# A two-layer hybrid decoder: S5 tables mirrored about their middle, modulation pages spread over the gates, small inputs joined, unread products in TensorE's waits

## The chip, the cores and the metric

The kernel runs on one core of a Trainium2 chip. The time is the device time of one execution in microseconds (us); the figure for a kernel is the median of its runs. Per instruction the trace gives start and duration on each engine: TensorE (PE, with its weight loads as PEld), VectorE (DVE), ScalarE (ACT), GpSimd (POOL), and SyncE (SP), which here only issues transfers.

## What is computed

The reference is a decoder trunk of two layers for 256 tokens of width 1024, in f32. Conditioning `c` gives six modulation vectors per layer; four token mixers run in parallel on slices of one input projection, are gated and merged; then comes a mixture of 16 experts with two chosen per token.

```python
def reference(x, c, positions, ada_w, ada_b, ...):
    c_act = jax.nn.silu(c)
    for l in range(DEPTH):
        mod = (c_act @ ada_w[l] + ada_b[l]).reshape(bsz, 6, 1, d)
        shift1, scale1, gate1, shift2, scale2, gate2 = (mod[:, i] for i in range(6))
        h = rmsnorm(x, mix_norm_g[l]) * (1.0 + scale1) + shift1
        u, q, k, v, iq, ik, iw, rg_x, rg_g, rw_f = _split(h @ w_in[l], IN_WIDTHS)
        # o_s5 (complex diagonal scan), o_dsa (top-k attention), o_rg (RG-LRU), o_rw (RWKV-7)
        up = jnp.einsum('btnw,nwd->btnd', branches, branch_w[l])
        gates = jax.nn.sigmoid(h @ gate_w[l] + gate_b[l]).reshape(bsz, seq, N_BRANCH, d)
        mixed = jnp.einsum('btnd,btnd->btd', gates, up) @ out_w[l]
        x = x + gate1 * mixed
        h2 = rmsnorm(x, ffn_norm_g[l]) * (1.0 + scale2) + shift2
        x = x + gate2 * moe(h2, router_w, router_b, exp_w1[l], exp_w3[l], exp_w2[l])
    return rmsnorm(x, final_norm_g)
```

The S5 scan needs the cosine and sine of 0 to 255 multiples of an angle for each state; these are the "tables".

## The kernel before

Weights come as pages of 128 x 2048 f32 (1 MB) through SyncE's queue, in one list written out ahead (`order`): the modulation pages of group 0 of layer 0 and `x`, then per layer the weights of the mixers, the pages of the fill plan, the output projection and the experts. A page is requested as soon as a buffer is free, from a ring of 5 and from a pool of 15 pages that work tiles share.

A weight that is multiplied in f32 is split into a high and a low part by `halves` (L598 to L601: ScalarE copies, VectorE subtracts), and `three` (L626 to L646) makes three matmuls of it; their line in the trace is L633 or L635.

The work of a layer is written as Python generators that a loop steps in turn (L1706 to L1757): `rwkv`, `others` (DSA, then S5, then RG-LRU) and, in layer 0, `s5_tables`. Beside them it steps `fill`, once the tables are there: two steps per chain step, later 1 and 3. `fill` (L1284 to L1309) follows `fill_plan` (L178 to L190), a string of 20 marks: a digit is a gate (48 matmuls of 128x256, then a tanh on ScalarE, L1309), a letter is the merge of a branch (L1311 to L1340). Ahead of each gate stand modulation pages: three in layer 0, whose list is groups 1 and 2 of the layer and then group 0 of the next, and two in layer 1. A scheduler then orders each engine's instructions by when they can run; an engine runs its own in order.

`ada` (L467 to L497) multiplies one modulation page. For groups marked `EARLY`, (0,0) and (1,0), TensorE does it (L480) into one of three PSUM banks tagged "acc", kept until the group's eighth page. For the others ScalarE scales the first page (L486) and VectorE adds each later one in four operations (L488). The addend `ada_b` has four rows of 512; GpSimd clears a 128x512 tile (L473) and ScalarE's queue loads the rows into it (L474). With the eighth page the sum is turned and stored as shift, scale and gate (`mod_values`, L516; `ada_rows` with L513).

`s5_tables` (L719 to L749) doubles the tables on GpSimd: from n entries come the next n, for n of 1, 2, 4 to 128, with six operations of 128 x 8n each (L731 to L736) and the doubled angle in five small ones (L740 to L744). Layer 0's runs as a chain at the start; layer 1's is stepped through in layer 0's `experts` (L1570 to L1654, at L1632 to L1634), between the fifth and the sixth of eight expert pairs.

`experts` gathers the tokens of a pair (L1532, L1536), multiplies by w1 and w3 (L1592), forms the SwiGLU (L1499, L1500), turns the result (`turn`, copied by ScalarE at L1511), multiplies by w2 (L1614) and adds the weighted result back in `combine` (L1563, L1564). `route` (L1432 to L1494) ranks the experts on VectorE and counts the tokens of each in five small matmuls (`pk`, L1457 to L1461).

Of the kernel before, what the change touches and what calls it, by code (L numbers as in the profile page):

```python
# [13 lines left out]
I32 = mybir.dt.int32  # L14
# [43 lines left out]
NMAT = _o  # L58

# [87 lines left out]
def _emit(ctx, tc, I, out):  # L147
# [30 lines left out]
    def fill_plan(l):  # L178

        groups = [(l, 1), (l, 2)] + ([(l + 1, 0)] if l + 1 < L else [])  # L180
        adas = [("ada", ll, g, kt) for ll, g in groups for kt in range(KT)]
        plan, k, ng, seen = [], 0, len(groups), [0] * 4
        for c in PLAN:
            if c.isdigit():
                plan += adas[k:k + ng] + [("gate", l, seen[int(c)], int(c))]
                k += ng
                seen[int(c)] += 1
            else:
                plan.append(("br", l, "abcd".index(c)))
        return plan  # L190
# [72 lines left out]

    def row(name, n):
        return bass.AP(tensor=I[name].tensor, offset=I[name].offset, ap=[[0, P], [1, n]])

    cols = []
    for l in range(L):
        c = ct(f"cols{l}", [P, NCOL])
        nc.scalar.dma_start(c, I["cols"][l])  # L270
        cols.append(c)
# [5 lines left out]
    pos_i = ct("pos_i", [P, 2], I32)  # L277
    nc.scalar.dma_start(pos_i, I["pos"])
    freq = ct("freq", [P, 48])
    nc.scalar.dma_start(freq, row("freq", 48))  # L280
    rtb = ct("rtb", [P, NE])
    nc.scalar.dma_start(rtb, row("router_b", NE))
    rtw = ct("rtw", [P, KT, NE])
    nc.scalar.dma_start(rtw, I["router_w"])
# [182 lines left out]
    def ada(l, g, kt):  # L467


        early = (l, g) in EARLY  # L470
        if kt == 0:
            b = M.take([P, 512])
            G.memset(b, 0.0)  # L473
            nc.scalar.dma_start(b[0:P:32, :], I["ada_b"][l, g])  # L474
            part[l, g] = b, pt("acc", [P, 512]) if early else M.take([P, 2048])
        b, p = part[l, g]
        w = get(("ada", l, g, kt))
        if early:
            for j in range(4):
                PE.matmul(p[32 * j:32 * j + 32, :], csil[:, kt, :], w[:, 512 * j:512 * j + 512],  # L480
                          start=kt == 0, stop=kt == KT - 1)
        else:
            for j in range(4):
                js = slice(512 * j, 512 * j + 512)
                if kt == 0:
                    S.activation(p[:, js], w[:, js], AF.Copy, scale=csil[:, kt, 0:1])  # L486
                else:
                    V.scalar_tensor_tensor(p[:, js], w[:, js], csil[:, kt, 0:1], p[:, js], op0=OP.mult, op1=OP.add)  # L488
        done(("ada", l, g, kt))
        if kt == KT - 1:  # L490
            if not early:
                a, p = p, pt("acc", [P, 512])
                for j in range(4):
                    PE.matmul(p[32 * j:32 * j + 32, :], ones_f[:, 0:32], a[:, 512 * j:512 * j + 512], start=True, stop=True)
                M.free(a)
            V.tensor_tensor(b, p, b, OP.add)
            mod_values(l, g, b)  # L497
# [10 lines left out]
    def ada_rows(o, r, j0):  # L508

        for j in range(2):  # L510
            p = pt("mx", [P, 512])
            q = slice(32 * (j0 + j), 32 * (j0 + j) + 1)
            PE.matmul(p, ones_f[q, :], r[q, :], start=True, stop=True)  # L513
            S.activation(o[:, 512 * j:512 * j + 512], p, AF.Copy, scale=0.5)
# [204 lines left out]
    def s5_tables(l, tabs):  # L719

        cs, sn = M.take([P, 8, T]), M.take([P, 8, T])
        tt = M.take([P, 8, P])
        G.memset(cs[:, :, 0:1], 1.0)
        G.memset(sn[:, :, 0:1], 0.0)
        ec, es = cs5[:, l], sn5[:, l]
        n = 1
        while n < T:
            t1, sh = tt[:, :, 0:n], [P, 8, n]
            ecb, esb = bc(ec[:, :, None], sh), bc(es[:, :, None], sh)
            c0, s0, c1, s1 = cs[:, :, 0:n], sn[:, :, 0:n], cs[:, :, n:2 * n], sn[:, :, n:2 * n]  # L730
# [6 lines left out]
            if 2 * n < T:  # L737
                e2 = sm("s5e2", [P, 2, 8])
                t2 = sm("s5t2", [P, 8])
                G.tensor_tensor(t2, es, es, OP.mult)  # L740
                G.tensor_tensor(e2[:, 0], ec, ec, OP.mult)
                G.tensor_tensor(e2[:, 0], e2[:, 0], t2, OP.subtract)
                G.tensor_tensor(t2, ec, es, OP.mult)
                G.tensor_scalar(e2[:, 1], t2, 2.0, None, op0=OP.mult)  # L744
                ec, es = e2[:, 0], e2[:, 1]
            n *= 2
            yield
        M.free(tt)
        tabs += [cs, sn]  # L749
# [682 lines left out]
    def route(l, lg):  # L1432
# [22 lines left out]

        pk = pt("mx", [P, 3, NE])
# [4 lines left out]
        PE.matmul(pk[:, 2], ones_b, mb[:, 1], start=False, stop=True)  # L1461
# [94 lines left out]
    def combine(x, oh, yh, yl, ss=None):  # L1556

        for a in range(2):
            for f in range(2):
                fs = slice(512 * f, 512 * f + 512)  # L1560
                p = pt("acc", [P, 512])
                for y in (yh, yl):
                    PE.matmul(p, oh[:, P * a:P * a + P], y[:, fs], start=y is yh, stop=y is yl)  # L1563
# [6 lines left out]
    def experts(l, x, oh, sid, wts, used, regi, gate2, beside):  # L1570
# [74 lines left out]
        if l + 1 < L:  # L1645
            return [rstd(ss, a) for a in range(2)]
# [62 lines left out]
    for kt in range(KT):  # L1709
        ada(0, 0, kt)  # L1710
    for l in range(L):
# [49 lines left out]
def layout(i):  # L1761
# [4 lines left out]
    o["pos"] = f("positions").reshape(2, P).T  # L1766
    o["ada_w"] = f("ada_w").reshape(L, KT, P, 3, 2048).transpose(0, 3, 1, 2, 4)
    o["ada_b"] = f("ada_b").reshape(L, 3, 4, 512)
# [25 lines left out]
    o["router_w"] = f("router_w").reshape(KT, P, NE).transpose(1, 0, 2)  # L1794
    o["router_b"] = f("router_b")
    o["final_g"] = f("final_norm_g")
    half = lambda n: np.float32(10000.0) ** (-np.arange(n, dtype=np.float32) / np.float32(n))
    o["freq"] = np.concatenate([half(32), half(16)]).astype(np.float32)
# [19 lines left out]
    o["cols"] = c  # L1818
# [36 lines left out]
```

## Time and profile before

| | before |
| --- | --- |
| median of 3 runs | 1219.07 us (1212.52 to 1219.73) |
| profiled execution | 1219.3 us |
| its span, first to last instruction | 1217.5 us |
| busy: TensorE, VectorE | 1087.1, 744.1 us |
| busy: ScalarE, GpSimd | 371.2, 230.0 us |
| bytes moved, mean rate | 329.82 MB, 271 GB/s |

The profile is of one execution. Idle time in front of an instruction is put down to what released it, its last semaphore. Matmuls are pipelined, so that the busy time of TensorE contains stretches in which it could take more. The granted clock is the share of full speed that TensorE had in a stretch.

### The profile page before, as it was taken

To read this page: it belongs to the slowest core of one execution; us is meant where nothing else is said; L and a number is where in the kernel's file an instruction comes from. 1 tells how busy PE (TensorE), PEld (TensorE's weight loads), DVE (VectorE), ACT (ScalarE), POOL (GpSimd) and SP (SyncE) were. 2 spreads that over 40 slices of the span, in tenths; PEclk is the share of its full clock that TensorE was granted. 3 is DMA by queue.
4 is the path that set the end of the run, shared out by engine and by line. 5 is a ranking of instruction groups with operands and counts; after the bars stand their busy time and mean duration, and the time that the engine had idled before them with its cause. 6 is when DMAs were issued, how large, how long until landed. Compare 5 with 4: busy or idle time off the path is not lost. (4 is left out here: it accounts for less than half of the span.)

```text
span 1217.5 us, 22749 instructions
## 1 busy us (share of the span) xinstructions
PE 1087.1 (89%) x9286; PEld 701.8 (58%) x9286; DVE 744.1 (61%) x1459; ACT 371.2 (30%) x663; POOL 230.0 (19%) x306
## 2 busy tenths in 40 slices
PE   4878999997988899999887999999898889999995
PEld 0867886865976433433227888987676633343331
DVE  5889995488776322423146889967987642243325
ACT  1643532421643110111016634433254311111112
POOL 0395211034140000009200031004524000000000
PEclk8988998998998899999898999999899989999998
DMA  8724785724566699999773467843156769999883
GB/s 358 280 100 170 281 313 209 310 104 160 221 222 229 244 418 421 419 422 380 298 307 107 171 243 291 300 174 139 40 203 223 295 235 419 420 420 421 357 348 163
DMA packets 47089, 329.82 MB, mean 271 GB/s; under 512 B 5993, under 2 KB 6121, under 8 KB 7553
## 3 DMA queue, kind: packets, MB, share of 16 engines
q1 hardware_dynamic: 45776, 327.47, 69.0%
q8 instruction: 78, 1.28, 0.4%
q10 hardware_dynamic: 1200, 0.79, 0.2%
q14 instruction: 35, 0.28, 0.1%
HBM read 327.19 MB, written 1.05 MB: 270 GB/s over the span
## 5 line engine op out<-in xcount | busy, mean ns | idle before, releaser
L633 PE MATMUL acc<-h_hi,whi 128*128 128x256 f32 x720 | 213.3, 296 | 0.0
L633 PE MATMUL acc<-h_hi,wlo 128*128 128x256 f32 x720 | 206.2, 286 | 5.9 <-DVE wlo L601 5.9
L633 PE MATMUL acc<-h_lo,whi 128*128 128x256 f32 x720 | 205.8, 286 | 0.7 <-DVE h_lo L601 0.7
L600 ACT ACTIVATE whi<-ring 128x1024 fp32r<-128x1024 f32 (+2 forms) x122 | 126.0, 1034 | 205.3 <-PE acc L633 132.7
L601 DVE TENSOR_TENSOR wlo<-ring,whi 128x1024 fp32r<-128x1024 f32 (+2 forms) x122 | 154.2, 1268 | 54.7 <-ACT whi L600 49.9
L633 PEld LDWEIGHTS acc<-h_hi,whi 128*128 128x128 f32 x720 | 139.6, 194 | 17.3 <-issue 10.4
L633 PEld LDWEIGHTS acc<-h_hi,wlo 128*128 128x128 f32 x720 | 139.8, 194 | 9.4 <-DVE wlo L601 7.7
L633 PEld LDWEIGHTS acc<-h_lo,whi 128*128 128x128 f32 x720 | 139.6, 194 | 4.6 <-issue 3.4
L1592 PE MATMUL rw<-page,page 128*32 (+1 forms) x736 | 92.3, 594 | 0.0
L488 DVE SCALAR_TENSOR_TENSOR page<-ring,csil,page 128x512 f32<-128x512 f32 x112 | 83.0, 777 | 1.1 <-DMA ring<-in_ada_w 1.1
L1592 PE MATMUL acc<-page,page 128*32 128x512 f32 (+1 forms) x688 | 82.0, 602 | 0.7 <-DVE page L1536 0.7
L1564 DVE TENSOR_TENSOR page<-page,acc 128x512 f32<-128x512 f32 x64 | 42.3, 684 | 54.8 <-PE acc L1563 54.7
L1614 PE MATMUL mx<-page,page 128*32 128x512 f32 (+1 forms) x560 | 65.7, 607 | 7.0 <-ACT page L1511 6.9
L1623 DVE SCALAR_TENSOR_TENSOR page<-mx,moslw,page 128x512 f32<-128x512 f32 x32 | 24.0, 751 | 74.5 <-PE mx L1614 73.0
L1536 DVE TENSOR_SCALAR page<-mx,scale,shift 128x256 f32<-128x256 f32 x32 | 17.4, 543 | 80.1 <-PE mx L1532 80.0
L600 ACT ACTIVATE wlo<-page 128x512 fp32r<-128x512 f32 x32 | 20.2, 631 | 129.1 <-DVE page L1623 120.0
L1534 ACT ACTIVATE page<-mx,shift,scale 128x256 f32<-128x256 f32 x32 | 18.0, 563 | 124.9 <-PE mx L1532 114.5
L1614 PE MATMUL mx<-ring,page 128*32 (+1 forms) x464 | 54.1, 601 | 0.7 <-ACT page L1511 0.7
L1592 PEld LDWEIGHTS rw<-page,page 128*32 128x32 f32 x736 | 24.4, 110 | 51.4 <-issue 49.5
L1563 PE MATMUL acc<-wlo,whi 128*128 128x512 f32 x128 | 43.6, 438 | 11.0 <-PEq L1602 5.7
L1336 POOL TENSOR_TENSOR page<-page,page 128x512 f32<-128x512 f32 x22 | 33.6, 1547 | 74.9 <-DVE page L1334 74.9
L1592 PEld LDWEIGHTS acc<-page,page 128*32 128x32 f32 x688 | 19.8, 110 | 43.4 <-issue 36.9
(521 smaller groups left out, 2097.8 us busy)
## 6 DMA issues: line engine op xcount, KB each, us to landing
page<-in_w SPq DMA_DIRECT2D x124, 1024.0 KB, 11.9
ring<-in_w SPq DMA_DIRECT2D x68, 1024.0 KB, 10.4
ring<-in_ada_w SPq DMA_DIRECT2D x45, 1024.0 KB, 5.7
ring<-in_gate_w SPq DMA_DIRECT2D x32, 1024.0 KB, 5.0
ring<-in_branch_w SPq DMA_DIRECT2D x8, 1024.0 KB, 4.8
ring<-in_w_rw SPq DMA_DIRECT2D x6, 1024.0 KB, 10.7
ring<-in_w_tm SPq DMA_DIRECT2D x6, 1024.0 KB, 4.8
ring<-in_w_fm SPq DMA_DIRECT2D x6, 1024.0 KB, 4.9
```

What stands on the lines that cost most here:

```text
L488: V.scalar_tensor_tensor(p[:, js], w[:, js], csil[:, kt, 0:1], p[:, js], op0=OP.mult, op1=OP.add)
L600: S.activation(hi, a, AF.Copy)
L601: V.tensor_tensor(lo, a, hi.bitcast(F32), OP.subtract)
L633: PE.matmul(p, w, x_, **f)
L1336: G.tensor_tensor(mix[dp], mix[dp], t, OP.add)
L1534: S.activation(xg[:, kt], p, AF.Identity, scale=sc[:, kt:kt + 1], bias=sh[:, kt:kt + 1])
L1536: V.tensor_scalar(xg[:, kt], p, sc[:, kt:kt + 1], sh[:, kt:kt + 1], op0=OP.mult, op1=OP.add)
L1563: PE.matmul(p, oh[:, P * a:P * a + P], y[:, fs], start=y is yh, stop=y is yl)
L1564: V.tensor_tensor(x[:, a, fs], x[:, a, fs], p, OP.add)
L1592: PE.matmul(hh[f][32 * g:32 * g + 32, :], xg[:, kt, P * i + 32 * g:P * i + 32 * g + 32], w[:, ds(offs[g] + 512 * f, 512)], start=kt == 0, ...
L1614: PE.matmul(yp[f][32 * g:32 * g + 32, :], gT[:, ft, 32 * g:32 * g + 32], w[:, ds(offs[g] + 512 * f, 512)], start=ft == 0, stop=ft == 3)
L1623: V.scalar_tensor_tensor(t, yp[f], o["w"][:, i:i + 1], gate2[:, fs], op0=OP.mult, op1=OP.mult)
```

## The change

1. `s5_tables`: the tables are built upwards from their middle, column 128, which holds the angle 0. Doubling runs for n of 1 to 64 only; the last step's doubled angle gives column 0. Two ScalarE copies with a reversed read then fill columns 1 to 127 (the sine with its sign turned). The scratch tile `tt` has 512 instead of 1024 elements. The number of generator steps stays 8.
2. `fill_plan`: group 1's pages stand ahead of gates 0, 0, 1, 2, 3, 4, 5, 6; group 2's ahead of gates 7 to 14; group 0 of the next layer ahead of gates 1, 3, 5 to 15. The list of transfers follows.
3. The addends are padded on the host to 128 x 512 and loaded by one request on SyncE's queue; the clearing goes.
4. The two `cols`, positions, frequencies, router weights and router bias come as one tile `par` of 128 x 420, in one request on ScalarE's queue.
5. `warm(n)` issues n matmuls of 128x256 bf16 into a PSUM bank that nobody reads, kept in issue order behind the latest of some marked matmuls: 6 after each of the last four pages of the first group, 22 ahead of `pk` and 9 behind it in each layer, 30 after layer 0's last `combine`.

```diff
     def fill_plan(l):
-        groups = [(l, 1), (l, 2)] + ([(l + 1, 0)] if l + 1 < L else [])
-        adas = [("ada", ll, g, kt) for ll, g in groups for kt in range(KT)]
-        plan, k, ng, seen = [], 0, len(groups), [0] * 4
+        plan, n, seen = [], 0, [0] * 4
         for c in PLAN:
             if c.isdigit():
-                plan += adas[k:k + ng] + [("gate", l, seen[int(c)], int(c))]
-                k += ng
+                for ll, g, at in ((l, 1, (0, 0, 1, 2, 3, 4, 5, 6)), (l, 2, range(7, 15)), (l + 1, 0, range(1, 16, 2))):
+                    if ll < L:
+                        plan += [("ada", ll, g, kt) for kt in range(KT) if at[kt] == n]
+                plan.append(("gate", l, seen[int(c)], int(c)))
+                n += 1
...
+    def warm(n):
+        p = pt("rw", [P, 512])
+        with tc.issue_after(state["pe"].ins):
+            for _ in range(n):
+                PE.matmul(p[:, 0:256], ones_b, slots, start=True, stop=True)
...
+    par = ct("par", [P, NPAR])
+    nc.scalar.dma_start(par, I["par"])
...
             b = M.take([P, 512])
-            G.memset(b, 0.0)
-            nc.scalar.dma_start(b[0:P:32, :], I["ada_b"][l, g])
+            nc.sync.dma_start(b, I["ada_b"][l, g])
...
     def s5_tables(l, tabs):
         cs, sn = M.take([P, 8, T]), M.take([P, 8, T])
-        tt = M.take([P, 8, P])
-        G.memset(cs[:, :, 0:1], 1.0)
-        G.memset(sn[:, :, 0:1], 0.0)
+        tt = M.take([P, 8, 64])
+        G.memset(cs[:, :, P:P + 1], 1.0)
+        G.memset(sn[:, :, P:P + 1], 0.0)
         ec, es = cs5[:, l], sn5[:, l]
         n = 1
-        while n < T:
+        while n < P:
...
-            c0, s0, c1, s1 = cs[:, :, 0:n], sn[:, :, 0:n], cs[:, :, n:2 * n], sn[:, :, n:2 * n]
+            c0, s0, c1, s1 = cs[:, :, P:P + n], sn[:, :, P:P + n], cs[:, :, P + n:P + 2 * n], sn[:, :, P + n:P + 2 * n]
...
+            last = 2 * n == P
+            ec2, es2 = (cs[:, :, 0], sn[:, :, 0]) if last else (e2[:, 0], e2[:, 1])
...
         M.free(tt)
+        S.activation(cs[:, :, 1:P], cs[:, :, T - 1:P:-1], AF.Copy)
+        S.activation(sn[:, :, 1:P], sn[:, :, T - 1:P:-1], AF.Copy, scale=-1.0)
+        yield
         tabs += [cs, sn]
...
+        warm(22)
         pk = pt("mx", [P, 3, NE])
...
-        PE.matmul(pk[:, 2], ones_b, mb[:, 1], start=False, stop=True)
+        state["pe"] = PE.matmul(pk[:, 2], ones_b, mb[:, 1], start=False, stop=True)
+        warm(9)
...
         combine(x, *outs.pop(NPAIR - 1), ss)
         if l + 1 < L:
+            warm(30)
             return [rstd(ss, a) for a in range(2)]
...
     for kt in range(KT):
         ada(0, 0, kt)
+        if kt >= 4:
+            warm(6)
```

## Rows read from the trace of the kernel before

**Rows 1.** The page's first part: busy us, share of the span, instructions.
```profile
PE 1087.1 (89%) x9286; PEld 701.8 (58%) x9286; DVE 744.1 (61%) x1459; ACT 371.2 (30%) x663; POOL 230.0 (19%) x306
```

**Rows 2.** Busy time by stretch: stretch, length, each engine, clock, DMA share, GB/s.
```profile
20.00:30.00 10.00, 6.50 (x28) 0.81 (x32) 8.03 (x59) 2.53 (x7) 0.52 (x1) 0.51 1.01 421
90.00:100.00 10.00, 6.49 (x40) 6.29 (x40) 9.87 (x9) 6.15 (x9) 10.00 (x7) 0.74 0.41 134
110.00:180.00 70.00, 67.79 (x961) 61.64 (x959) 67.64 (x124) 31.65 (x61) 13.04 (x11) 1.00 0.75 282
190.00:200.00 10.00, 7.85 (x40) 3.97 (x38) 4.33 (x9) 2.92 (x6) 1.15 (x2) 0.71 0.28 100
250.00:340.00 90.00, 80.25 (x546) 64.46 (x545) 76.00 (x105) 31.61 (x49) 31.09 (x28) 0.94 0.45 163
390.00:400.00 10.00, 2.34 (x11) 1.19 (x10) 8.37 (x47) 1.74 (x3) 0.00 (x0) 0.50 0.11 47
440.00:570.00 130.00, 127.05 (x1048) 49.18 (x1037) 43.93 (x78) 18.76 (x32) 21.05 (x65) 1.00 1.01 420
580.00:590.00 10.00, 4.32 (x24) 1.04 (x28) 1.37 (x2) 1.08 (x2) 4.84 (x3) 0.67 0.90 380
```

**Rows 3.** Timeline of GpSimd in layer 0's experts: start, duration, operation (idle before).
```profile
572.97 1.27 POOL L736 TENSOR_TENSOR page<-page,page 128x512 f32<-128x512 f32 x1
...
582.66 2.34 POOL L736 TENSOR_TENSOR page<-page,page 128x1024 f32<-128x1024 f32 x1
```

**Rows 4.** Timeline of ScalarE in the experts, layer 0 and layer 1.
```profile
421.49 0.60 ACT L1499 ACTIVATE page<-acc 128x512 f32<-128x512 f32 x1 [3.06 <-PE acc L1592]
...
585.03 0.60 ACT L1511 ACTIVATE page<-acc 128x512 f32<-128x512 f32 x1 [14.23 <-POOL page L736]
...
1001.55 0.60 ACT L1499 ACTIVATE page<-acc 128x512 f32<-128x512 f32 x1 [3.06 <-PE acc L1592]
...
1157.11 0.60 ACT L1511 ACTIVATE page<-acc 128x512 f32<-128x512 f32 x1 [7.38 <-PE acc L1509]
```

**Rows 5.** The page's costliest groups: operation, count, busy us, mean ns, idle before.
```profile
L600 ACT ACTIVATE whi<-ring 128x1024 fp32r<-128x1024 f32 (+2 forms) x122 | 126.0, 1034 | 205.3 <-PE acc L633 132.7
```

**Rows 6.** Timeline of GpSimd in the first stage of layer 0.
```profile
84.16 1.89 POOL L732 TENSOR_TENSOR page<-page,s5e 128x1024 f32<-128x1024 f32 x1
...
98.60 2.74 POOL L736 TENSOR_TENSOR page<-page,page 128x1024 f32<-128x1024 f32 x1
```

**Rows 7.** Lines L856, L888: count: ns min/median/max, first (layer 0), last (layer 1) start.
```profile
L856 DVE COPY page<-rwrn x2: 426/1252/2077, 89.5 to 696.8; 128x512 f32<-128x512 f32 x2
...
L888 DVE TENSOR_TENSOR page<-page,rw x2: 676/681/686, 104.9 to 702.1; 128x512 f32<-128x512 f32 x2
```

**Rows 8.** Groups by line: L488 in the whole span, then 110 to 180 alone.
```profile
L488 DVE SCALAR_TENSOR_TENSOR page<-ring,csil,page 128x512 f32<-128x512 f32 x112 | 83.0, 777 | 1.1 <-DMA ring<-in_ada_w 1.1
...
L488 DVE SCALAR_TENSOR_TENSOR page<-ring,csil,page 128x512 f32<-128x512 f32 x49 | 36.1, 772 | 0.0
...
L633 PE MATMUL acc<-h_hi,whi 128*128 128x256 f32 x105 | 30.9, 294 | 0.0
```

**Rows 9.** Timeline of TensorE within a gate, at full clock.
```profile
186.03 0.28 PE L633 MATMUL acc<-h_lo,whi 128*128 128x256 f32 x1
186.15 0.28 PE L633 MATMUL acc<-h_hi,wlo 128*128 128x256 f32 x1
```

**Rows 10.** Timeline of TensorE at layer 0's router and the gather behind it.
```profile
389.02 2.07 PE L513 MATMUL mx<-page,ones_f 1*128 1x512 f32 x2
396.44 0.20 PE L1457 MATMUL mx<-momb,before 128*128 128x16 bf16 x1 [5.35 <-DVE momb L1452]
...
400.55 0.41 PE L1532 MATMUL mx<-whi,h_hi 128*128 128x256 f32 x1
400.76 0.41 PE L1532 MATMUL mx<-whi,h_lo 128*128 128x256 f32 x1
```

**Rows 11.** Timeline of VectorE at the start.
```profile
10.97 0.25 DVE L660 TENSOR_SCALAR page<-freq,posf 128x48 f32<-128x48 f32 x1 [1.67 <-DMA freq<-in_freq]
```

## What the change will do to the time

> **What bounds the kernel now.** Over the whole run TensorE is busy 1087.1 of 1217.5 us [rows 1], but that average hides stages with different limits, so I read the busy time by stage next [rows 2]. At 110–180 (RWKV and the first gates) VectorE is busy 67.6 of 70 us and TensorE 67.8, which is no clean verdict, since matmul busy time is modelled with pipelining. At 90–100 GpSimd is busy 10.0 of 10, VectorE 9.87, TensorE 6.49 at a granted clock of 0.74: the two vector engines set the pace. At 250–340 (the S5 and RG-LRU scans) VectorE has 76.0 of 90. At 440–570, the experts, the DMA share is 1.01 at 420 GB/s: there no engine matters, only transfers. But at 580–590, still among the experts, TensorE drops to 4.32 of 10 and the DMA share to 0.90. At 390–400, the router, VectorE works alone (8.37) and TensorE's clock is 0.50, its 1.2 GHz level. Then I read single instructions around these places [rows 3 to 11].
>
> **Tables in layer 0's experts (A).** The layer-1 tables are built on GpSimd while layer 0's experts run. The change drops the last doubling step, six operations of 128x1024. Their stretch runs from the end of the previous 512-wide step (572.97 + 1.27 = 574.24) to 582.66 + 2.34 = 585.00, i.e. 10.8 us here [rows 3]. Right there ScalarE's L1511, which copies expert activations, waits 14.23 us for the page that this last L736 frees, and starts at 585.03 [rows 4]. Layer 1 has no table building: its first L1499 is at 1001.55 against 421.49, and the same L1511 at 1157.11. The distance is 155.56 us there and 163.54 here, so the stall is 8.0 us net of what layer 1 waits there anyway. It can't be absorbed by transfers, because SyncE's page requests stop in it too (the DMA share falls, above), and the stage is bound by bytes. What is added are two ScalarE copies of 128 x 1016 in reversed order; the nearest row is a 128x1024 copy at 1.03 us [rows 5], so 2.1 us on an engine that was idle, done at about 574.3 + 2.1 = 576.4, just before 577.1 (421.49 + 155.56), when L1511 would be ready. The reversed read is not in the trace: if each copy took twice that, 4.1 us, L1511 would come 1.4 us late. Bounds: gain of 4 (half, the transfers being late from before) to 14.2 (the whole wait). I take **−8**.
>
> **Tables in layer 0's start (B).** The same step runs there from 84.16 (its first L732) to 98.60 + 2.74, its six operations taking 14.1 us, longer than in the other set [rows 6]. VectorE is slowed meanwhile: the copy L856 takes 2077 ns against 426 for the same copy in layer 1, and from L856 to L888 pass 104.9 − 89.5 = 15.4 us against 702.1 − 696.8 = 5.3 [rows 7]. So 10.1 us are lost over the stretch. Without the step GpSimd's last 512-wide operation ends near 87.3, before most of it. What takes its place is again 2.1 us on ScalarE, which is busy 6.15 of 10 here [rows 2]. The clock at 90–100 is 0.74, so TensorE is no bound there. Bounds: 5 (half the stretch is then bound by weight conversion, L600 and L601) to 14.1. I take **−10**. The Trainium skill, "SBUF — State Buffer", section "Who interferes with whom", says that VectorE and GpSimd share a port pair as an exclusive lock held for a whole instruction, and that whoever issues first makes the other block entirely. By that rule all of GpSimd's 14.1 us could come off VectorE's path, and the sum would be 4 lower; L856's two durations agree with the rule, but the times from L856 to L888 say 10.
>
> **Modulation pages spread (C).** A layer has 14 pages that VectorE multiplies (seven each of groups 1 and 2; the eighth of each is on ScalarE). L488 takes 777 ns, four to a page: 3.1 us a page, 112 of them 83.0 us [rows 8]. Before, all 14 come within the first six gates in layer 0 and the first eight in layer 1; 49 of these operations, 36.1 us, lie within 110–180 [rows 8]. Afterwards group 2's pages come ahead of gates 7 to 14. So 7 pages, 21.7 us a layer, leave a stretch in which VectorE is busy 67.6 of 70. About two of them land beside gates 8 and 9, where VectorE is half idle (4.33 of 10 at 190–200), and five, 15.5 us, at 250–340, where it has 14 us free of 90, but mostly at the end of that stretch. TensorE and ScalarE follow closely in the first stage: a matmul of L633 is listed with 0.28 us but they issue 0.12 apart [rows 9], and the stage has 3 x 105 of them [rows 8] among 961 matmuls [rows 2]: 37.8 us, and 646 others, mostly 64 columns wide, for which I estimate a quarter of that spacing each, 19 us. That leaves TensorE perhaps 13 to 15 us of 70, and no more than that can be gained. Taking −15 for what leaves, +10 for what comes back within the scans (15.5 less a third that finds idle time), I get −5 in layer 0 and −2 in layer 1, where only groups 1 and 2 exist and the order changes less: **−7**. The pages of layer 1's group 0 go to TensorE; they hold one of three accumulation banks from gate 1 to 15 instead of gates 5 to 7. A gate needs one bank at a time, so I cost this at 0, with +4 if evictions and the next gate collide. Bounds: −30 (TensorE's 15 us in each layer, nothing back) to +31 (two times 15.5 back, nothing gained).
>
> **Unread products (D).** Between L513's end (389.02 + 2.07) and L1457 at 396.44 TensorE is idle 5.35 us; the gather after it runs at half clock, matmuls 0.21 apart [rows 10]. 22 matmuls of that size at 0.21 are 4.6 us: they fit into the gap even at half clock. At full clock the gather's ten or so matmuls that follow would come at half the distance, about 1.1 us per layer. The other places are the first pages (clock 0.51 at 20–30, but DMA share 1.01, so hardly 0.7) and the end of layer 0, about 1 us. Sum **−3**; bounds −4.5 to +0.5 (the products running into L1457). The Trainium skill, "TensorE: Matmul & The Clock Gate", section "The mechanism", says that matmuls start and end in program order, so L1457 can't overtake an unread one. That would cost 22 × 0.21 − 5.35 < 0 by the row, so nothing.
>
> **Small inputs (E).** Six memsets go from GpSimd and six requests from ScalarE's queue; one request for 215 KB takes the place of six, and the padded addends go onto SyncE's queue, behind which the weight pages wait in order: 0.26 MB at 421 GB/s is 0.6 us each, of which two fall into stretches bound by bytes (20–30 and 110–180). VectorE waited 1.67 us for the frequencies, landing singly; with one larger request it may wait 1 us more, ahead of the first page's product [rows 11]. Both together **0**, bounds −1 to +2.
>
> **Sum.** −8 − 10 − 7 − 3 + 0 = −28. The profiled execution took 1219.3 us, 0.2 from the median of the runs: 1219.3 − 28 = 1191.
>
> **Rivals.** (1) The spread nets nothing: TensorE or the conversions L600 and L601 already hold the first stage; C = 0, time 1198. For it: TensorE's 67.8 of 70. (2) It pays in full and GpSimd's whole hold comes off: C = −17, B = −14: 1219.3 − 8 − 14 − 17 − 3 = 1177; below that lies the bound of C. For it VectorE's 67.6 of 70; against it, TensorE's close second. (3) Slower: the five late pages of each layer fall into the scans, where VectorE is the bound, and the first stage doesn't shrink. That is +31 against A, B and D's −21: 1229. It decides from two thirds of the moved time (21 of 31) showing. Against it: VectorE's 14 idle us in 250–340. (4) The tables were hidden anyway: A is given back to the transfers, and in B the conversions and the two ScalarE copies, queued behind them, take the place: 1219.3 − 7 − 3 = 1209. For it ScalarE's 6.15 of 10 in that stretch; against it, L1511's wait and L888's lag. That the unread products raise no clock is D = 0, which alone moves any of these by 3.
>
> **How the numbers follow.** Forecast 0.48, (1) 0.20, (2) 0.10, (3) 0.10, (4) 0.12. A measurement of this kernel can tell about 1% from no change, so the bounds are 1207 and 1231. Faster: nearly all of the forecast (0.45), most of (1) (0.17), (2) 0.10, a third of (4) (0.04): 0.76. Same: the rest of these, 0.03 + 0.03 + 0.08, and a little under half of (3): 0.18. Slower: 0.06. The range runs from 1172 (a little below (2)) to 1212 (above (4)); outside it are (3) and some of (2) and (4), about 0.18. The forecast alone lies within 1183 to 1200.
>
> **What would show it.** A: L1511's 14 us wait is gone, and from the first L1499 to it pass about 156 us. B: L856 near 0.43 us and L856 to L888 under 8. C: VectorE's share at 110–180 falls while the gates there come earlier; if the gates keep their times, (1) holds, and if the scans at 250–340 grow by 10 us or more, (3). D: a clock above 0.5 in the gather. What would break the sum most is the instruction order shifting as a whole: stages that meet different neighbours than in these rows.

## The result and the profile after

| | before | after |
| --- | --- | --- |
| median | 1219.40 us (1212.52 to 1220.28, 4 runs) | 1261.38 us (1257.50 to 1262.27, 4 runs) |
| ratio to before | | 1.0346, 95% interval 1.0307 to 1.0385 |
| span of the profiled execution | 1217.5 us | 1260.5 us |

The changed kernel is 3.5% slower, 42 us, where 28 less was forecast. The lines of the changed kernel are shifted: L488 of before is L499 in it, L494 is L505, L600 and L601 are L611 and L612, L633 is L644, L856 and L888 are L871 and L903, L1052 is L1067, L1499 is L1516, L1511 is L1528, L1592 is L1609. The two new copies are L761 and L762.

The page's first part, as in [rows 1]:

```profile
PE 1124.4 (89%) x9402; PEld 733.4 (58%) x9402; DVE 731.2 (58%) x1459; ACT 374.8 (30%) x667; POOL 191.8 (15%) x288
```

GpSimd has 38 us less work, as the change says, and VectorE takes 13 us less for the same 1459 instructions. TensorE is busy 37 us longer, with 116 unread products more and at a mean granted clock of 0.938 against 0.948. The span grew by 43 us all the same, so waits have to be looked for. Busy time by stretch of the changed kernel, as in [rows 2] (stretch, length, PE, PEld, DVE, ACT, POOL, clock, DMA share, GB/s):

```profile
20.00:30.00 10.00, 9.18 (x63) 3.40 (x55) 7.26 (x46) 1.00 (x2) 0.00 (x0) 0.87 1.02 419
60.00:80.00 20.00, 6.11 (x29) 4.43 (x27) 0.72 (x1) 5.46 (x8) 18.19 (x51) 0.59 0.11 43
110.00:180.00 70.00, 70.00 (x940) 64.07 (x940) 60.35 (x102) 30.20 (x55) 9.34 (x8) 1.00 0.75 287
...
560.00:580.00 20.00, 8.88 (x55) 4.29 (x55) 4.01 (x8) 4.15 (x6) 8.49 (x15) 0.61 0.31 129
857.00:978.00 121.00, 100.47 (x621) 81.13 (x619) 96.16 (x130) 35.86 (x56) 41.66 (x35) 0.84 0.40 151
```

Two stretches stand out that have no counterpart before. At 60–80 VectorE works 0.72 of 20 us (before: 16.31) and only GpSimd is busy for most of it; at 560–580, in the stage that was bound by transfers, the DMA share is 0.31. Both hold the same picture. The timeline of ScalarE there (start, duration, operation, idle before it and what ended that):

```profile
73.82 1.05 ACT L761 ACTIVATE page<-page 128x1016 f32<-128x1016 f32 x1 [16.68 <-POOL page L744]
74.78 0.40 ACT L813 ACTIVATE page<-page 32x256 f32<-32x256 f32 x1
...
565.77 1.05 ACT L761 ACTIVATE page<-page 128x1016 f32<-128x1016 f32 x1 [19.62 <-POOL page L744]
568.32 1.05 ACT L762 ACTIVATE page<-page 128x1016 f32<-128x1016 f32 x1 [1.50 <-POOL page L747]
569.28 1.13 ACT L611 ACTIVATE wlo<-page 128x512 fp32r<-128x512 f32 x2
```

A copy takes 1.05 us, as estimated from the row of L600. But ScalarE stood 16.68 and 19.62 us in front of it: the copy is in ScalarE's queue ahead of L813, L611 and the expert copies, which had nothing to do with the tables, and it waits for GpSimd's last doubling step. What stood behind, on VectorE, TensorE and SyncE:

```profile
79.28 1.23 DVE L612 TENSOR_TENSOR wlo<-ring,whi 128x1024 fp32r<-128x1024 f32 x1 [21.46 <-ACT whi L611]
...
75.23 0.79 PE L828 MATMUL rw<-page,page 32*128 32x256 f32 x1 [13.42 <-ACT page L813]
...
569.92 0.69 DVE L612 TENSOR_TENSOR wlo<-page,wlo 128x512 fp32r<-128x512 f32 x1 [15.89 <-ACT wlo L611]
...
571.12 1.93 PE L1609 MATMUL acc<-page,page 128*32 x7 [16.30 <-DVE page L1553]
...
551.94 0.42 SPq L236 DMA_DIRECT2D page<-in_w  x1
585.68 0.33 SPq L236 DMA_DIRECT2D ring<-in_w  x1
```

These are rows of the timelines of VectorE and TensorE (at the start, then in the experts) and of SyncE. SyncE requested no page for 585.68 − 551.94 = 33.7 us; that is the DMA share of 0.31. Before, the longest pause there was 572.57 − 555.99 = 16.6 us:

```profile
555.99 0.42 SPq L228 DMA_DIRECT2D page<-in_w  x1
572.57 0.33 SPq L228 DMA_DIRECT2D ring<-in_w  x1
```

The experts of layer 0 lost 14.7 us in all. 11.3 of them lie in the distance from the first L1499 (now L1516) to the L1511 of [rows 4] (now L1528), which was 163.54 us and is 593.97 − 419.15 = 174.82:

```profile
419.15 0.60 ACT L1516 ACTIVATE page<-acc 128x512 f32<-128x512 f32 x1 [3.06 <-PE acc L1609]
...
593.97 0.60 ACT L1528 ACTIVATE page<-acc 128x512 f32<-128x512 f32 x1 [7.44 <-PE acc L1526]
...
1043.68 0.60 ACT L1516 ACTIVATE page<-acc 128x512 f32<-128x512 f32 x1 [3.06 <-PE acc L1609]
```

Along the run the changed kernel lags behind the one before as follows, by the same instruction in both traces:

| place | lag, us |
| --- | --- |
| layer 0: L856 (copy in RWKV), 105.0 against 89.5 | +15.5 |
| layer 0: first S5 scan, 241.8 against 253.1 | −11.3 |
| layer 0: last merge, 354.6 against 357.3 | −2.8 |
| layer 0: first L1499 of the experts, 419.1 against 421.5 | −2.3 |
| layer 0: last round of `combine`, 650.0 against 637.6 | +12.4 |
| layer 1: L856, 712.3 against 696.8 | +15.5 |
| layer 1: first S5 scan, 857.1 against 837.5 | +19.6 |
| layer 1: last merge, 977.8 against 937.3 | +40.5 |
| layer 1: first L1499, 1043.7 against 1001.5 | +42.1 |

So four places count: the start of layer 0, where 15 us are lost and made up; layer 0's experts, +15; layer 1's first stage, +7 from the last round of `combine` to the first scan; and layer 1 between its first scan and its last merge, +21. The 7 us stay open: of the parts run alone, the inputs lose 4 us in that stage, the others 1 at most. The rows of the last place, from VectorE's timeline of the kernel before and of the changed one:

```profile
837.49 1.17 DVE L1196 TENSOR_TENSOR_SCAN page<-s5r,page 128x256 f32<-128x256 f32 x1
...
937.33 0.67 DVE L1334 SCALAR_TENSOR_TENSOR page<-page,acc 128x512 f32<-128x512 f32 x1
```

```profile
857.12 1.20 DVE L1211 TENSOR_TENSOR_SCAN page<-s5r,page 128x256 f32<-128x256 f32 x1 [0.62 <-POOL page L1208]
...
977.79 0.67 DVE L1349 SCALAR_TENSOR_TENSOR page<-page,acc 128x512 f32<-128x512 f32 x1
```

### The profile page after: what moved, and what is told of

Same layout as the page of the kernel before. It is cut to its first block, busy times and chain, and to the rows that moved or that the text cites. A ratio compares the mean times of both kernels' runs of the same rounds, so it can differ in the third digit from the quotient of the medians.

```text
span 1260.5 us, 22941 instructions
## 1 busy us (share of the span) xinstructions
PE 1124.4 (89%) x9402; PEld 733.4 (58%) x9402; DVE 731.2 (58%) x1459; ACT 374.8 (30%) x667; POOL 191.8 (15%) x288
## 3 DMA queue, kind: packets, MB, share of 16 engines
HBM read 328.72 MB, written 1.05 MB: 262 GB/s over the span
## 5 line engine op out<-in xcount | busy, mean ns | idle before, releaser
L644 PE MATMUL acc<-h_hi,whi 128*128 128x256 f32 x720 | 218.6, 304 | 2.1 <-DVE page L1349 2.1
L644 PE MATMUL acc<-h_hi,wlo 128*128 128x256 f32 x720 | 210.7, 293 | 2.2 <-DVE wlo L612 2.1
L644 PE MATMUL acc<-h_lo,whi 128*128 128x256 f32 x720 | 209.2, 291 | 1.7 <-DVE h_lo L612 1.7
L611 ACT ACTIVATE whi<-ring 128x1024 fp32r<-128x1024 f32 (+2 forms) x118 | 121.7, 1032 | 233.7 <-PE acc L644 194.7
L612 DVE TENSOR_TENSOR wlo<-ring,whi 128x1024 fp32r<-128x1024 f32 (+2 forms) x118 | 143.5, 1218 | 77.7 <-ACT whi L611 77.2
L644 PEld LDWEIGHTS acc<-h_hi,whi 128*128 128x128 f32 x720 | 142.4, 198 | 21.8 <-issue 12.1
L644 PEld LDWEIGHTS acc<-h_hi,wlo 128*128 128x128 f32 x720 | 142.5, 198 | 10.0 <-DVE wlo L612 4.5
L644 PEld LDWEIGHTS acc<-h_lo,whi 128*128 128x128 f32 x720 | 142.8, 198 | 3.9 <-DVE h_lo L612 2.2
L1609 PE MATMUL acc<-page,page 128*32 128x512 f32 (+1 forms) x672 | 82.6, 618 | 16.6 <-DVE page L1553 16.6
L1609 PE MATMUL rw<-page,page 128*32 (+1 forms) x736 | 93.8, 600 | 0.0
L499 DVE SCALAR_TENSOR_TENSOR page<-ring,csil,page 128x512 f32<-128x512 f32 x112 | 87.4, 806 | 5.0 <-DMA ring<-in_ada_w 5.0
L611 ACT ACTIVATE wlo<-page 128x512 fp32r<-128x512 f32 x32 | 20.1, 630 | 124.1 <-DVE page L1640 115.0
L1351 POOL TENSOR_TENSOR page<-page,page 128x512 f32<-128x512 f32 x24 | 39.2, 1652 | 104.9 <-DVE page L1349 104.9
L1609 PEld LDWEIGHTS acc<-page,page 128*32 128x32 f32 x672 | 19.9, 112 | 59.1 <-issue 38.3
L1609 PEld LDWEIGHTS rw<-page,page 128*32 128x32 f32 x736 | 24.2, 111 | 51.0 <-issue 49.3
L1631 PE MATMUL mx<-ring,page 128*32 x464 | 53.2, 593 | 0.7 <-ACT page L1528 0.7
## 6 DMA issues: line engine op xcount, KB each, us to landing
ring<-in_w SPq DMA_DIRECT2D x69, 1024.0 KB, 12.4
```

The source lines that it names most:

```text
L611: S.activation(hi, a, AF.Copy)
L612: V.tensor_tensor(lo, a, hi.bitcast(F32), OP.subtract)
L644: PE.matmul(p, w, x_, **f)
L1351: G.tensor_tensor(mix[dp], mix[dp], t, OP.add)
L1609: PE.matmul(hh[f][32 * g:32 * g + 32, :], xg[:, kt, P * i + 32 * g:P * i + 32 * g + 32], w[:, ds(offs[g] + 512 * f, 512)], start=kt == 0, ...
L1631: PE.matmul(yp[f][32 * g:32 * g + 32, :], gT[:, ft, 32 * g:32 * g + 32], w[:, ds(offs[g] + 512 * f, 512)], start=ft == 0, stop=ft == 3)
```

## The experiments

Theory 1: the two ScalarE copies stand in its in-order queue far ahead of their tables. Theory 2: group 2's pages, moved to gates 7 to 14, come late in the scans' stage, with the matmuls that close the group. Rivals: the late tables hold the stages whoever copies; the loss comes from the small inputs, the addends on SyncE's queue, the unread products, or the order shifting as a whole. Each median stands beside runs of the kernel before on the same chip (1217.8, 1218.1, 1217.8 and 1222.2 us), and the ratio is to those.

**The copies on GpSimd, in the changed kernel.**

```diff
-        S.activation(cs[:, :, 1:P], cs[:, :, T - 1:P:-1], AF.Copy)
-        S.activation(sn[:, :, 1:P], sn[:, :, T - 1:P:-1], AF.Copy, scale=-1.0)
+        G.tensor_scalar(cs[:, :, 1:P], cs[:, :, T - 1:P:-1], 1.0, None, op0=OP.mult)
+        G.tensor_scalar(sn[:, :, 1:P], sn[:, :, T - 1:P:-1], -1.0, None, op0=OP.mult)
```

> The changed kernel with the two mirror copies moved from ScalarE to GpSimd (two tensor_scalar, by 1 and by -1); all else as changed. Theory 1 (the two ScalarE copies stand in that engine's in-order queue far ahead of the tables they need, and everything behind them waits: 16.7 us at 57-74 and 19.6 us at 546-566 in the changed kernel): both waits go, ScalarE's conversions and expert copies run on; the layer-0 experts get back their 15 us and the start a part of its 15: 1261 falls to about 1238 (1228 to 1246). Rival (the tables themselves are what the stages need, whoever copies): the waits reappear as waits for GpSimd's copies and the time stays within 1255 to 1265.

Measured 1249.73 us, ratio 1.0281 (1.0228 to 1.0335): neither. Layer 0's experts came out right: the kernel enters them 2.6 us behind the one before and leaves them 1.8 us ahead. But the start lost more, 22.4 us at L856. GpSimd's and VectorE's timelines there:

```profile
77.25 2.76 POOL L761 TENSOR_SCALAR page<-page 128x1016 f32<-128x1016 f32 x1
...
86.63 0.24 DVE L1071 TENSOR_TENSOR page<-page 128x80 f32<-128x80 f32 x1 [22.35 <-POOL page L1067]
```

Now VectorE waits 22.35 us, for the rotary product L1067, which stands behind the tables in GpSimd's queue; VectorE's own queue had this L1071 ahead of everything else. A copy takes GpSimd 2.76 us against ScalarE's 1.05. So the wait moved to another in-order queue: theory 1 holds for the experts, and its rival is right about the start.

**The old fill plan, in the changed kernel.**

```diff
-                for ll, g, at in ((l, 1, (0, 0, 1, 2, 3, 4, 5, 6)), (l, 2, range(7, 15)), (l + 1, 0, range(1, 16, 2))):
...
+        groups = [(l, 1), (l, 2)] + ([(l + 1, 0)] if l + 1 < L else [])
...
+                plan += adas[k:k + ng] + [("gate", l, seen[int(c)], int(c))]
```

> The changed kernel with the old fill plan (modulation pages in the first gates, groups one after another); all else as changed. Theory 2 (layer 1 loses its 25 us between the scans and the last merge because the last pages of group 2, and TensorE's closing matmuls for them, stand among gates 13 to 15): the distance from layer 1's S5 scan to its last merge falls from 74 to about 55 us and the time from 1261 to about 1238 (1230 to 1248). Rival (that loss comes from the addends on SyncE's queue or the one request of small inputs, or from the order shifting in general): 1253 to 1263.

Measured 1233.26 us, ratio 1.0147 (1.0095 to 1.0198). In layer 1 the lag changes from +11.0 at the first scan to +11.4 at the last merge: nothing is lost there any more, as theory 2 has it, and the total is in its range.

**The mirrored tables alone, on the kernel before.** `s5_tables` of the change, nothing else.

> The kernel before with the mirrored tables and their ScalarE copies alone. Theory 1: ScalarE stalls as in the changed kernel, some 15 us more in layer 0's experts instead of 8 less, and 0 to 15 at the start: 1228 to 1248, about 1236. Rival (the stall comes only in company with the other parts): faster than before, 1200 to 1212.

Measured 1230.62 us, ratio 1.0133 (1.0075 to 1.0190). The stall needs no company:

```profile
ACT page L750 <- POOL page L733: 19.6, 1, 19.6
PEld acc L1596 <- DVE page L1540: 16.5, 1, 16.5
```

That is its list of waits at 540–590 (engine, line, waited for: us in total, times, longest). The mixers of layer 0 come out 5.6 us ahead of before, the experts lose 13.

**The spread alone, on the kernel before.** `fill_plan` of the change, nothing else.

> The kernel before with the new fill plan alone. Theory 2: layer 0's first stage gains some 10 us and gives it back by its last gates, layer 1 gains nothing in its first stage and loses 20 to 25 us behind its scans: 1235 to 1246, about 1240. Rival (the spread pays and the loss comes from elsewhere): 1205 to 1218.

Measured 1238.53 us, ratio 1.0198 (1.0134 to 1.0262). The first S5 scan of layer 0 comes 13.3 us earlier and its last merge 2.0 later; in layer 1 the first scan is level (−0.1) and the last merge 15.4 late.

**The copies where S5 begins, on the kernel before.** Mirrored tables, with the copies taken out of `s5_tables` and put into `s5`:

```diff
         cs, sn = tabs
+        with tc.issue_after(state["dsa"].ins):
+            S.activation(cs[:, :, 1:P], cs[:, :, T - 1:P:-1], AF.Copy)
+            S.activation(sn[:, :, 1:P], sn[:, :, T - 1:P:-1], AF.Copy, scale=-1.0)
```

Here `state["dsa"]` is ScalarE's last copy in DSA.

> The kernel before with the mirrored tables, but the two ScalarE copies are issued behind the last ScalarE copy of DSA, where S5 begins, in each layer. Theory 1 (what costs in the mirrored form is where the copies stand in ScalarE's queue): no wait of ScalarE for a table is left; layer 0's experts come out 4 to 8 us faster than before, instead of 13 slower with the copies at once; the start of layer 0 still has VectorE waiting for the first rotary product behind GpSimd's tables, made up by the end of the mixers; total 1204 to 1214, about 1208. Rival (the gap in the experts comes from the pages that the tables hold and from GpSimd's late tables): experts no faster than before, 1217 to 1232.

Measured 1225.88 us, ratio 1.0043 (1.0015 to 1.0071). The profiled execution's ScalarE has no wait for a table left, and the L1511 of [rows 4] comes 584.16 − 427.47 = 156.69 us behind the first L1499, close to the 155.56 of layer 1:

```profile
427.47 0.60 ACT L1503 ACTIVATE page<-acc 128x512 f32<-128x512 f32 x1 [3.06 <-PE acc L1596]
...
584.16 0.60 ACT L1515 ACTIVATE page<-acc 128x512 f32<-128x512 f32 x1 [7.47 <-PE acc L1513]
```

The experts gained 5.4 us, as theory 1 expected. But the total missed, and lies in the range of the rival, whose own condition, experts no faster than before, did not come true: the start of layer 0 and the scans lost 5.9, and 3.5 more went between layer 1's last gates and its experts. At the start the same wait as with GpSimd's copies shows, 5 us shorter (list of waits at 60–110):

```profile
DVE page L1057 <- POOL page L1053: 17.5, 1, 17.5
```

**Group 2's pages earlier, on the kernel before.** The new plan with one line changed:

```diff
-                for ll, g, at in ((l, 1, (0, 0, 1, 2, 3, 4, 5, 6)), (l, 2, range(7, 15)), (l + 1, 0, range(1, 16, 2))):
+                for ll, g, at in ((l, 1, (0, 0, 1, 2, 3, 4, 5, 6)), (l, 2, (5, 6, 6, 7, 7, 8, 9, 10)), (l + 1, 0, range(1, 16, 2))):
```

> The kernel before with the new fill plan, except that group 2's pages stand ahead of gates 5, 6, 6, 7, 7, 8, 9, 10 instead of 7 to 14; group 1 and the next layer's group 0 as in the change. Theory 2 (the loss is the three late pages of group 2, 12 VectorE operations and their closing matmuls among gates 13 to 15 behind the scans): the scans' stage goes back to about 100 us from first scan to last merge in both layers, the first stage keeps some of its gain: 1207 to 1219, about 1213. Rival (the loss comes from the accumulation bank held by layer 1's group 0, or from the ring's look-ahead whatever the group): layer 1 still loses 10 us or more, 1230 to 1240; the bank can only show in layer 0.

Measured 1219.70 us, ratio 0.9995 (0.9967 to 1.0022). Against the late pages that is 2% less for the same 16 pages a layer. The last merge comes 5 us ahead of before in layer 0 and level in layer 1 (+0.4), and behind the first scan VectorE multiplies no page of group 2 any more, in either layer. Theory 2 holds for these 2%, but not for all that comes back behind the scans. From the first scan to the last merge pass 111.2 us in layer 0 and 106.7 in layer 1, where about 100 were expected (before: 104.3 and 99.8; with the late pages: 119.5 and 115.3). VectorE's rows in layer 1, with the late pages and with the early ones:

```profile
837.39 1.20 DVE L1197 TENSOR_TENSOR_SCAN page<-s5r,page 128x256 f32<-128x256 f32 x1 [0.62 <-POOL page L1194]
...
952.72 0.68 DVE L1335 SCALAR_TENSOR_TENSOR page<-page,acc 128x512 f32<-128x512 f32 x1
```

```profile
831.08 1.18 DVE L1197 TENSOR_TENSOR_SCAN page<-s5r,page 128x256 f32<-128x256 f32 x1
...
937.74 0.68 DVE L1335 SCALAR_TENSOR_TENSOR page<-page,acc 128x512 f32<-128x512 f32 x1
```

So 7 us a layer of what the first stage gains come back without a late page; why is open. Layer 0 still holds the accumulation bank from gate 1 to 15 here and gains, so the bank is not what costs.

**The unread products alone, on the kernel before.**

> The kernel before with the unread products alone. Forecast of the prediction: -3 us, the gather behind the router at full clock: 1212 to 1219. Rival (they stand in TensorE's way or change the instruction order): 1219 to 1226.

Measured 1216.40 us, ratio 0.9982 (0.9954 to 1.0009): no change that can be told. The profiled execution is 1.7 us ahead in layer 0's experts and level again by layer 1's start.

**The inputs alone, on the kernel before.** One request for the small inputs, padded addends.

> The kernel before with the padded addends on SyncE's queue and the one request of small inputs alone. Forecast of the prediction: 0, between -1 and +2: 1217 to 1222. Rival (the wait for a free tile ahead of the addend's request holds up the weight pages on SyncE's queue): 1225 or more.

Measured 1219.95 us, ratio 1.0007 (0.9980 to 1.0035), as forecast; the rival needed 1225 or more.

**Mirrored tables with late copies in layer 1 only.** Layer 0 keeps the full doubling.

> The kernel before with mirrored tables for layer 1 only, their two ScalarE copies issued where layer 1's S5 begins; layer 0 keeps its full tables at the start. Theory 1: layer 0's start is as before (VectorE no longer waits 17 us for the rotary product behind GpSimd's shortened tables, as it did with both layers mirrored), the experts of layer 0 keep their 5 us gain: 1209 to 1215, about 1212. Rival (the 17 us are only a shift, and the 6 us that the mixers lost came from the later copies at S5): layer 0's mixers as before, but layer 1 gains nothing or loses what the experts gave: 1216 to 1222.

Measured 1219.99 us, ratio 1.0017 (0.9990 to 1.0044), in the rival's range. The start is level with before (L856 −0.5 us), so the 17.5 us do belong to the shortened tables there. The L1511 of [rows 4] comes 571.61 − 414.85 = 156.76 us behind the first L1499, 6.8 less than before. But the last `combine`, which started its last round at 637.56 before, starts at 633.21: only 4.3 ahead, having entered 6.6 ahead. From L1511 to there pass 61.6 us instead of 52.5, so the 6.8 gained were given back with 2.3 more. ScalarE's, VectorE's and TensorE's timelines, and below them two rows by stretch:

```profile
414.85 0.60 ACT L1540 ACTIVATE page<-acc 128x512 f32<-128x512 f32 x1 [3.05 <-PE acc L1633]
...
571.61 0.60 ACT L1552 ACTIVATE page<-acc 128x512 f32<-128x512 f32 x1 [7.46 <-PE acc L1550]
...
633.21 0.68 DVE L1605 TENSOR_TENSOR page<-page,acc 128x512 f32<-128x512 f32 x1
...
589.72 2.90 PE L1604 MATMUL acc<-wlo,whi 128*128 128x512 f32 x6 [5.35 <-PEq L1643]
```

```profile
580.00:590.00 10.00, 4.65 (x41) 1.54 (x34) 2.22 (x4) 1.66 (x3) 0.00 (x0) 0.88 1.01 421
590.00:600.00 10.00, 8.51 (x36) 2.98 (x39) 2.75 (x4) 0.20 (x1) 0.00 (x0) 0.61 0.68 258
```

At 580–590 TensorE is busy 4.65 of 10 us while the transfers run at full rate, with no table on the way. That speaks for the prediction's fourth rival, as far as the experts go. The row behind TensorE's idle time names its own sequencer (a branch, L1643), so which page was late, if one was, is open.

**Both repairs in the changed kernel.** Copies where S5 begins, group 2's pages at gates 5 to 10.

> The changed kernel with the two repairs: copies at the start of S5 in each layer, group 2's pages ahead of gates 5 to 10. Theory 1 and 2 together account for the slowdown: what is left is the sum of the single runs, +6 (mirror, late copies), +2 (spread, early), 0 (unread products), +3 (inputs), 1218 + 11 = 1229 at most, and with the gains of the experts 1215 to 1230. Rival (some 13 us of the slowdown belong to none of the parts and come from their company): 1235 to 1245.

Measured 1224.02 us, ratio 1.0065 (1.0040 to 1.0089): 2.8% of the 3.5% come back.

**Layer 1's tables late, the early spread in layer 0 alone.**

> The kernel before with layer 1's mirrored tables and late copies, and the early spread in layer 0 alone (layer 1 keeps two pages a gate). Theory: the gains add, 5 us in layer 0's experts and 5 in layer 0's mixers: 1204 to 1212, about 1208. Rival (gains of single parts don't add, the instruction order decides): 1213 to 1222.

Measured 1216.26 us, ratio 0.9982 (0.9955 to 1.0010). The rival was right. The first L1499 of layer 0 comes 12.8 us earlier than before (408.70 against 421.49), that of layer 1 only 2.3 (999.24 against 1001.55): 3 us go in layer 0's last expert pairs, 5 in layer 1's first stage, 2 behind its scans.

**The same with unread products and inputs.**

> As the run before, with the unread products, the padded addends and the one request of small inputs added. Theory: these give 0 to -4 in layer 0 and lose as much by layer 1: within 4 us of that run, 1204 to 1214. Rival (their company with the spread costs, as in the changed kernel): 8 us or more above it.

Measured 1214.96 us, ratio 0.9975 (0.9954 to 0.9996). It is the fastest version found, by a quarter of a per cent, its whole interval just under 1.

**One repair at a time in the changed kernel, and the two costly parts together.** The profiled spans of the four parts add up to 30 us, that of the change to 43; three runs on that.

> The changed kernel with group 2's pages ahead of gates 5, 6, 6, 7, 7, 8, 9, 10. If the 13 us belong to the late pages: it falls to the level of the changed kernel with the old plan, 1229 to 1238. If they belong to the copies or to the company of the small parts: it gives back only the 16 us that the spread costs alone, 1242 to 1250.

Early pages: 1240.05 us, ratio 1.0127 (1.0073 to 1.0181). In layer 1 the lag goes from +16.2 at the first scan to +19.9 at the last merge, instead of from +19.6 to +40.5.

> The changed kernel with the two copies issued where S5 begins. If the 13 us belong to the late pages: only what the copies cost is given back, some 15 in the experts: 1243 to 1250. If they belong to the copies: 1228 to 1238.

Late copies: 1242.01 us, ratio 1.0161 (1.0107 to 1.0216). The experts go from +3.0 to −2.2; layer 1's scans still lose 14.5 us.

> The kernel before with the mirrored tables (copies as in the change) and the new fill plan, without the unread products and the inputs. If these two alone make the excess: 1252 to 1263, as the changed kernel. If it needs the small parts: the sum of the two, 1241 to 1249.

Mirror and spread on the kernel before: 1257.33 us, ratio 1.0277 (1.0226 to 1.0328). By ratios the parts add up: 1.33 + 1.98 = 3.31% for these two, whose interval is 2.26 to 3.28, and with −0.18 and +0.07 for the others 3.20% against the 3.46 measured (3.07 to 3.85). The excess of 13 us stood in the profiled spans (30 for the four parts, 43 for the change); in the timed runs it is within what the intervals leave open. The first two of these three runs fell between the ranges that were given for them, the third into the one for an excess made by mirror and spread alone. The sizes that were expected rested on the spans and decide nothing between them.

## Why the prediction was wrong

By the runs of the single parts, A and B together were forecast at −18 us and gave +16 (1.33% of 1218); C −7 and gave +24; D −3 and gave −2; E 0 and gave +1 (these last two within their intervals of 0). So the signs of A with B and of C were wrong, and in both the wait of an instruction in its engine's queue was left out of the sum.

**A, the experts' tables: the mechanism was seen, the sign was lost in the copies.** The stall of L1511 was there and belonged to the tables: with the copies out of the way the distance of 163.54 fell to 156.7, 6.8 us against the 8 forecast. The step that failed is "2.1 us on an engine that was idle". ScalarE was idle at 574 because its next instruction was waiting; where the copies would stand in its order was not asked. The instruction order put them ahead of the conversions (what made it do so, no run shows), and ScalarE waited 19.62 us. The price named what runs beside the copies, not what is queued behind them. The Trainium skill, "PSUM — Partial Sum Buffer", section "Engine vs sequencer instructions", says that ScalarE's, VectorE's and GpSimd's queues are strictly first in, first out. The rows of L761 with L813 behind it agree, and this is the rule that should have stood against the term. A second part of the step fell as well, "can't be absorbed by transfers": where layer 0 came into the experts earlier (layer 1's tables late), the last two pairs took 9 us more and gave the gain back. With late copies in both layers, where the experts were entered 6 us late, they took 1.4 more and most of the gain stayed.

**B, the start: right in its cause, wrong in what comes next.** VectorE is freed of GpSimd's slowing: L856 takes 419 to 427 ns in both layers, and 4.7 us pass from it to L903, against 15.4 before [rows 7]:

```profile
L871 DVE COPY page<-rwrn x2: 419/423/427, 105.0 to 712.3; 128x512 f32<-128x512 f32 x2
...
L903 DVE TENSOR_TENSOR page<-page,rw x2: 676/679/682, 109.7 to 717.4; 128x512 f32<-128x512 f32 x2
```

That is 10.7 us gained, and L856 itself comes 15.5 late. Both signs that the prediction named (L856 near 0.43, under 8 us to L888) came true, in a kernel that gained nothing at this place: they were signs inside the stretch, and the wait lay in front of it. Without ScalarE's early copies (copies on GpSimd, or late in both layers) the wait of VectorE on GpSimd's first rotary product took ScalarE's place, so that L856 came 15 to 22 us late in every form of the shorter tables that was run in layer 0. By the last merge most of that is made up: the mixers end 6 us early with the copies at once and 6 late with late copies. How much of these 6 is the tables' is open, for layer 0's mixers also end 4 to 7 us early where the tables of layer 0 are as before (inputs alone, layer 1's tables late).

**C, the spread: rival 3 in layer 1, with three of its five pages and a second cost.** In the first stage VectorE's time fell as forecast, 67.6 to 60.35 of 70, and layer 0's first scan came 11 to 13 us early, of which the forecast had 15. But layer 1 gained nothing there (−0.1 alone). What came back was mis-sized: three pages lie behind the first scan, not five, 12 operations and 9.7 and 10.7 us in the two layers. Behind its first scan layer 1 loses 15 us with the spread alone and 21 in the change; 7 of them come back with the early pages too, so 8 to 9 of the 15 belong to the late pages and what closes their group. VectorE at 857–978 grouped by line (count, busy us, mean ns, idle before), and then VectorE's, TensorE's and ScalarE's timelines:

```profile
L499 DVE SCALAR_TENSOR_TENSOR page<-ring,csil,page 128x512 f32<-128x512 f32 x12 | 10.7, 909 | 0.0
```

```profile
937.31 1.75 DVE L499 SCALAR_TENSOR_TENSOR page<-ring,csil,page 128x512 f32<-128x512 f32 x1
...
939.12 1.91 PE L505 MATMUL acc<-page,ones_f 128*32 128x512 f32 x2 [4.55 <-DVE page L499]
...
950.16 1.06 ACT L611 ACTIVATE whi<-ring 128x1024 fp32r<-128x1024 f32 x1 [20.71 <-PE acc L644]
```

The part that was left out is L505, TensorE's closing matmul of a group. It stands in TensorE's order ahead of most of gate 15's matmuls and waits for the last L499, which ended at 937.31 + 1.75 = 939.06. After these 4.55 us without work TensorE has a granted clock of 0.50, its 1.2 GHz level, until 950, and ScalarE's next conversion waits 20.71 us for it:

```profile
939.00:950.00 11.00, 10.88 (x44) 9.22 (x45) 3.94 (x9) 0.00 (x0) 0.00 (x0) 0.50 0.88 331
940.00:960.00 20.00, 20.00 (x120) 18.46 (x118) 7.31 (x11) 6.54 (x8) 0.00 (x0) 0.72 0.70 263
```

By estimate the idle time and half of the 10.88 busy us make 10 us for TensorE here. The prediction moved only the four VectorE operations of each page, and not what ends a group. Ending the group four gates earlier took 2% back, with all else equal. How the loss divides between the 10.7 us of VectorE and TensorE's waits was not measured apart.

**D, the unread products: right at the router, in the end no change that can be told.** The 22 products take 4.87 us in the gap and `pk` still waits for VectorE, 0.55 us; the gather behind runs 0.12 apart instead of 0.21 [rows 10]:

```profile
389.58 4.87 PE L277 MATMUL rw<-slots,ones_b 128*128 128x256 bf16 x22
395.00 0.18 PE L1473 MATMUL mx<-momb,before 128*128 128x16 bf16 x1 [0.55 <-DVE momb L1467]
...
397.79 0.28 PE L1549 MATMUL mx<-whi,h_lo 128*128 128x256 f32 x1
397.91 0.28 PE L1549 MATMUL mx<-whi,h_hi 128*128 128x256 f32 x1
```

From L1457 to the experts' first L1499 the lag goes from −1.4 to −2.3 us, 0.9 gained where 1.1 was forecast. Alone they gave −0.2% within ±0.3, which holds both the forecast of −3 us and 0; in the profiled execution what was gained ahead of the experts was gone by layer 1's start. The three places of the term add up to 3.9 by the prediction's own figures (2.2, at most 0.7 and 1), not to 3.

**E, the inputs: right,** +0.07% within ±0.28.

**The chances.** Rival 3 gave 1229 and had 0.10; its place is where layer 1 lost, though in layer 0 the first stage did shrink. No case had the table part itself turning into a loss; rival 4 alone has the copies in a queue, but behind the conversions, and they stood ahead of them. The wait of another engine's queue behind an added instruction was in reach of the rows: L1511's 14.23 us behind L736 was such a wait already.

## What to carry to other kernels

An instruction that is added to an idle engine is priced by what stands behind it in that engine's queue when its input is late, and not by its own duration: here two pairs of copies, of 2.1 us each, had ScalarE stand for 36 us. A step that moves takes along every instruction up to its last consumer; the closing matmul of a group can hold up a queue that the moved work itself never touches. And a gain of 7 to 13 us in one stage is not a gain of the kernel until the next stage has been read.

## What the runs showed that was not expected

The two mirror copies with a reversed read take ScalarE 1.05 us each, no more than an ordinary copy of that size (1.03), but 2.76 us on GpSimd. With layer 1's tables late and the early spread in layer 0, the profiled execution's gain of 12.8 us at layer 0's experts shrank to 2.3 by layer 1's, with no single wait to show for it in the rows read; where exactly the 5 us in layer 1's first stage go stays open.
